# Weight buffers of a float32 decoder trunk at seven different places modulo 256 bytes

## The chip, the cores and the metric

The kernel runs on one core of a Trainium2 chip. A core has TensorE (PE in the profile; PEld is its loading of the stationary operand), VectorE (DVE), ScalarE (ACT), GpSimd (POOL) and SyncE (SP), which here only issues DMAs. Tiles lie in SBUF: 128 partitions, and along each partition a byte address that is the same for all of them. When this text speaks of the place of a tile, it means that address; "modulo 256" is its remainder. Matmul results lie in PSUM, a separate memory that the change does not touch.

The metric is the device time of one execution in microseconds (us). A profile is one execution recorded by the hardware profiler; its span goes from the first to the last instruction.

## The reference, cut to what matters

Four residual layers on 256 tokens of 1,024 channels, all in float32. Layer i uses the mixer A, B, C, A: gated spatial mixing, dilated attention in three groups, and causal pooling with a linear map by group. Every layer reads a large input projection and an output projection from HBM.

```python
def reference(x, ...):
    for i in range(DEPTH):
        kind, j = i % N_MIXERS, i // N_MIXERS
        h = rms_norm(x, norm_gain[i])
        if kind == 0:
            y = mixer_a(h, a_w_in[j], a_v_gain[j], a_w_s[j], a_b_s[j], a_w_out[j])
        elif kind == 1:
            y = mixer_b(h, b_w_in[j], b_q_gain[j], b_k_gain[j], b_w_out[j])
        else:
            y = mixer_c(h, c_w_in[j], c_w_grp[j], c_scale[j], c_w_out[j])
        x = x + y.astype(x.dtype)
    return x

def mixer_a(h, w_in, v_gain, w_s, b_s, w_out):
    proj = h @ w_in                       # u, v, z of 2,048 columns each
    ...
    y = u * mixed * jax.nn.silu(z)
    return y @ w_out
```

## The kernel before

**Products in three matmuls.** To reach float32 accuracy on a faster type (float32r), each operand is split in a high part (rounded by a ScalarE copy, `hi_of`, L82) and a low part (what is left, a VectorE subtraction, `lo_of`, L85). `mm3` (L75 to L79) then issues three matmuls into the same PSUM tile: high x high (L77), high x low (L78), low x high (L79). Each names a stationary operand first, which is loaded into the array, and a moving one, which streams through it.

**Weights as a stream of units.** The host orders all weights into 272 units of 128 partitions x 1,024 float32 (4,096 bytes a partition), in the order of use. `load_units` (L127) brings unit u by a DMA of SyncE into one of four raw buffers wr. `split_hi` (L137) takes a pair of tiles from the weight pool, one high and one low, and writes the high part; `split_units` (L147) writes the low part, after which the raw buffer is free for the load four units on. There are W_BUFS = 7 pairs, used in turn, and the splits run five units (AHEAD) ahead of the matmuls that read them. `next_unit` hands out unit u as wuh and wul.

**Who reads them.** `proj_tok` (v, z, u of layers A; qk and v01 of B; the first cz of C) keeps h stationary (hTh and hTl, 128 x 128 slices) and lets the weights move, 512 columns at a time: 12 matmuls a unit, called wide below. `proj_out` (wo, all layers) does the same with the layer's result y as the stationary operand: y0, y3 in layers A, yb in B, cy in C. `proj_feat` (bz in B; cz and cx in C) turns the roles: weight slices of 128 columns are stationary and 256 columns of h move, 24 matmuls a unit, called narrow. Layer C's `group` (cg) does that with the pooled differences cd in place of h, and the v2p products of layer B move 256 columns of weights over stationary h. The remaining products, mx in layers A and s and o in B, have no weight unit in them: both operands come from tiles of the layer.

**What sets the order.** Nothing is scheduled by cost: the Python program's order is the order on each engine. Small generator tasks (splits of h, attention steps, the transposes by a matmul with an identity, yp, qt, pt and hp) are woken by `tick`, which the projections call after each step, so they fall between matmuls at fixed places. Each engine waits by semaphores for the tiles that it reads and for the buffers that it overwrites.

**What sets the places.** Tiles lie in SBUF in the order in which pools and tags take room. First the pool of x, hTh, hTl, identity and constants, then the weight pool (four wr, seven high, seven low, each 4,096 bytes), and above it the pool of the layer that runs, taken anew for each layer. Within a tag the buffers follow one another without a gap, so all fourteen weight tiles stand at the same remainder.

Of the kernel before, what the change touches and what calls it, by code (L numbers as in the profile page):

```python
# [11 lines left out]
F32R = mybir.dt.float32r  # L12
# [5 lines left out]
P = 128  # L18
# [3 lines left out]
HALF = 512  # L22
# [14 lines left out]
UNIT = 1024  # L37
RAW_BUFS = 4
W_BUFS = 7
# [9 lines left out]
def hybrid_trunk_kernel(ctx, tc, x, wts, norm_gainT, a_v_gain, a_wsT, a_bsT, b_gl, b_gv, c_scaleT,  # L49
# [5 lines left out]
    wp = ctx.enter_context(tc.tile_pool(name="wp", bufs=1))  # L55
# [15 lines left out]
    def pair(pool, shape, tag, name, bufs):  # L71
        return (pool.tile(shape, F32R, tag=tag + "h", name=name + "h", bufs=bufs),
                pool.tile(shape, F32R, tag=tag + "l", name=name + "l", bufs=bufs))
# [7 lines left out]
    def hi_of(hi, src):  # L81
        nc.scalar.activation(hi, src, AF.Copy)  # L82
# [44 lines left out]
    def load_units(n):  # L127
        while loaded[0] < min(n, n_units):
            u = loaded[0]
            raw = wp.tile([P, 2, HALF], F32, tag="wr", name=f"wr{u}", bufs=RAW_BUFS)  # L130
            nc.sync.dma_start(raw, wts[u].rearrange("p (k n) -> p k n", n=HALF))
            raws.append(raw)
            loaded[0] += 1
# [3 lines left out]
    def split_hi(n):  # L137

        while split[0] < min(n, n_units):
            u = split[0]  # L140
            load_units(u + 1)
            hi, lo = pair(wp, [P, 2, HALF], "w", f"w{u}", W_BUFS)
            hi_of(hi, raws[u])
            units.append((hi, lo))
            split[0] += 1

    def split_units(n):  # L147

        split_hi(n)
        while lowered[0] < min(n, n_units):  # L150
            u = lowered[0]
            lo_of(units[u][1], raws[u], units[u][0])
            lowered[0] += 1
            load_units(u + 1 + RAW_BUFS)
# [8 lines left out]
    def step(i, ahead=AHEAD):  # L163

        tick()
        if i % 2 == 0:
            split_hi(used[0] + ahead)
        else:
            split_units(used[0] + ahead)
# [120 lines left out]
    def proj_out(layer, nkt, yT):  # L290
# [15 lines left out]
        for t in range(2):  # L306
            for i, (j, n, w) in enumerate(tail):
                for kk in range(2):
                    k = 2 * j + kk
                    mm3(acc[t][n], yT(k, t), (w[0][:, kk], w[1][:, kk]), False, k == nkt - 1)  # L310
                if t == 0 and nkt == 16 and i == 0:
                    split_units(used[0] + 3)
                if t == 0 and nkt != 16 and i == 2:
                    split_units(used[0] + 1)
                    split_hi(used[0] + 3)
                if t == 1 and i == 0:
                    split_units(used[0] + 4)
                if j == nkt // 2 - 1:
                    xh = xt[t][:, n * HALF:(n + 1) * HALF]
                    nc.vector.tensor_tensor(xh, acc[t][n], xh, op=ALU.add)  # L320
                    if layer == DEPTH - 1:
                        nc.sync.dma_start(out[t * P:(t + 1) * P, n * HALF:(n + 1) * HALF], xh)
                    elif t == 0:
                        half_ss(t, n, ss[t])
                if layer < DEPTH - 1 and i == 3:
                    if t == 0:
                        split_units(used[0] + 2)
                        spawn(norm_task(layer + 1, 0, ss))
                        split_units(used[0] + 3)
                    else:  # L330
                        for n in range(2):
                            half_ss(1, n, ss[1])
                tick()
# [712 lines left out]
```

## Time and profile before

| | |
|---|---|
| time, median of 2 runs | 850.48 us (850.07 and 850.89) |
| the profiled execution's own time | 850.76 us |
| its span | 849.1 us |
| granted TensorE clock, mean | 1.00 |
| DMA share of 16 engines, weight queue | 51.4% |
| HBM read | 147.72 MB |

The profiled execution lies 0.28 us above the median and its time 1.7 us above its span. In a row of the timeline stand the start in us, the duration in us, the engine, the line, the operation, the output, the operands, the shape and how many instructions the row holds. In a row of a group stand the line, the engine, the operation, output and operands with their shapes, the count, the busy time in us and the mean in ns, and then the idle time ahead of these instructions with what ended it. A matmul's duration overlaps that of the next one, so the interval between starts is what it costs in a stream.

Where the tiles stood modulo 256, from the built program (u is the number of the unit):

```
tile                                   before   after
x, ident, kc (v gain, w_s, masks)      128      128
wr (raw weights), hTh, hTl             0        0
wuh and wul, unit u                    0        32 * (u mod 7)
tiles of layers A: v, y, wsr, sz, yy   0        224
tiles of layer B: qk, p, pT, v01, yb   0        224
layer C: cd, szT, czs                  128      96
layer C: cy, cdd, cyy                  0        224
```

### The profile page before, as it was taken

What the parts mean: (1) busy time and instruction counts of PE and PEld (TensorE: products, weight loads), DVE (VectorE), ACT (ScalarE), POOL (GpSimd) and SP (SyncE); (2) the same over time, 40 slices, a digit from 0 to 9 for tenths busy, and PEclk for the clock granted to TensorE, in tenths of its full rate; (3) what the DMA queues carried; (4) which work ended last, traced back from release to release, by engine and by line L of the source; (5) the groups of instructions that cost most, each with busy time, mean ns of one, the idle gap of its engine ahead of it and who ended that gap; (6) DMA issues with size and microseconds to landing.
All of it is one profiled execution on the core that took longest, in us unless ns stands there. A gap on an engine that the chain in (4) does not pass through costs nothing.

```text
span 849.1 us, 12424 instructions
## 1 busy us (share of the span) xinstructions
PE 837.2 (99%) x4600; PEld 724.6 (85%) x4600; DVE 546.8 (64%) x932; ACT 488.9 (58%) x918; POOL 57.4 (7%) x79
## 2 busy tenths in 40 slices
PE   8999999999999999999999999999999999999998
PEld 6888888888988888888888889999988888888886
DVE  6876556646747567667667575797764777555551
ACT  7665444436668677677677566455443676434340
POOL 1301000001001011021021012000000000000000
PEclk9999999999999999999999999999999999999999
DMA  8766565562755346345345268447564376555541
GB/s 286 280 205 222 188 198 172 175 198 96 246 163 166 110 140 193 110 145 187 113 148 181 68 224 261 163 149 248 174 215 157 125 241 208 171 175 173 172 150 50
DMA packets 41500, 149.57 MB, mean 176 GB/s; under 512 B 4864, under 2 KB 4880, under 8 KB 41184
## 3 DMA queue, kind: packets, MB, share of 16 engines
q1 hardware_dynamic: 40320, 144.72, 51.4%
q0 software_dynamic: 976, 4.05, 1.5%
q8 instruction: 36, 0.59, 0.3%
q14 instruction: 24, 0.20, 0.1%
q10 hardware_dynamic: 144, 0.02, 0.0%
HBM read 147.72 MB, written 1.05 MB: 175 GB/s over the span
## 4 chain that ended last, share of the span: by engine, by line
PE 86%; ACT 7%; DVE 2%; issue 2%; POOL 2%; DMA 1%; SPq 0%; POOLq 0%; DVEq 0%
PE wo L77 6%; PE wo L79 6%; PE wo L78 6%; PE qk L77 4%; PE qk L78 4%; PE qk L79 4%; PE z L77 3%; PE z L79 3%; PE z L78 3%; PE u L77 3%; PE u L78 3%; PE u L79 3%; PE v L78 3%; PE v L79 3%; PE v L77 3%; ACT junk L499 2%
## 5 line engine op out<-in xcount | busy, mean ns | idle before, releaser
L504 POOL TENSOR_TENSOR qr<-qm,m 128x4 f32<-128x4 f32 x24 | 30.3, 1272 | 225.4 <-DVE qm L503 225.4
L508 ACT ACTIVATE qn<-qk,qr 128x128 f32<-128x128 f32 x96 | 27.5, 382 | 15.1 <-POOL qr L504 15.1
L499 ACT ACTIVATE junk<-qk 128x128 bf16<-128x128 f32 x96 | 26.8, 279 | 7.2 <-PE qk L79 4.5
L422 DVE TENSOR_TENSOR sz<-u,sz 128x512 f32<-128x512 f32 x16 | 11.0, 686 | 28.0 <-PE u L79 28.0
L225 ACT ACTIVATE hTh<-hp,gT 128x128 fp32r<-128x128 f32 x64 | 17.5, 382 | 16.0 <-PE hp L221 16.0
L206 POOL TENSOR_TENSOR r<-ms,m 128x1 f32<-128x1 f32 x8 | 5.4, 669 | 288.5 <-DVE ms L204 288.5
L320 DVE TENSOR_TENSOR x<-wo,x 128x512 f32<-128x512 f32 x16 | 11.0, 689 | 20.0 <-PE wo L79 20.0
L228 DVE SCALAR_TENSOR_TENSOR hTl<-hp,gT,hTh 128x128 fp32r<-128x128 f32 x64 | 17.9, 343 | 7.7 <-ACT hTh L225 7.7
L364 ACT ACTIVATE junk<-v 128x512 bf16<-128x512 f32 x16 | 9.6, 600 | 17.6 <-PE v L79 17.5
L499 ACT ACTIVATION_READ_ACCUMULATOR junk<-qk 128x1 f32 x96 | 19.1, 199 | 0.0
L365 DVE TENSOR_TENSOR vv<-v,kc 128x512 f32<-128x512 f32 x16 | 10.9, 689 | 12.1 <-ACT junk L364 12.0
L517 DVE TENSOR_TENSOR ra<-qn,kcb 128x64 f32<-128x64 f32 x48 | 10.6, 221 | 12.0 <-ACT qn L508 10.9
L448 ACT ACTIVATE sz<-z 128x512 f32<-128x512 f32 x16 | 9.5, 598 | 15.3 <-PE z L79 14.8
L529 PE MATMUL qt<-ident,qn 128*128 128x128 f32 x96 | 14.6, 274 | 3.5 <-DVE qk22l L537 0.6
L529 PEld LDWEIGHTS qt<-ident,qn 128*128 128x128 f32 x96 | 11.3, 140 | 7.3 <-issue 2.7
L199 ACT ACTIVATE junk<-x 128x512 bf16<-128x512 f32 x16 | 10.3, 643 | 10.7 <-DVE x L320 9.4
L425 DVE SCALAR_TENSOR_TENSOR yy<-mx,bs,sz 128x256 f32<-128x256 f32 x32 | 14.0, 480 | 0.6
L599 ACT ACTIVATE p<-p,rl 128x384 f32<-128x384 f32 (+1 forms) x16 | 11.5, 769 | 4.7 <-DVE rl L598 4.7
L521 DVE TENSOR_TENSOR rb<-qn,kcb 128x32 f32<-128x32 f32 x96 | 13.7, 184 | 0.0
L595 ACT ACTIVATE p<-p,nb 128x768 f32<-128x768 f32 x8 | 7.5, 939 | 8.0 <-DVE nb L594 8.0
L503 DVE TENSOR_SCALAR qm<-qs 128x4 f32<-128x4 f32 x24 | 3.3, 164 | 12.7 <-ACT junk L499 12.7
L345 POOL TENSOR_SCALAR_AFFINE_SELECT kc<-kc 128x128 f32<-128x128 f32 x16 | 9.8, 649 | 14.4 <-DMA kc<-in_a_wsT_dram 8.6
(2770 smaller groups left out, 3269.2 us busy)
## 6 DMA issues: line engine op xcount, KB each, us to landing
wr<-in_wts_dram SPq DMA_DIRECT2D x272, 512.0 KB, 3.8
kc<-in_a_v_gain_dram POOLq DMA_DIRECT2D x2, 1024.0 KB, 6.6
x<-in_x_dram SPq DMA_DIRECT2D x4, 256.0 KB, 4.8
kc<-in_a_wsT_dram POOLq DMA_DIRECT2D x2, 512.0 KB, 8.3
out_dram<-x SPq DMA_DIRECT2D x4, 256.0 KB, 2.0
kcb<-in_masks_dram POOLq DMA_DIRECT2D x1, 576.0 KB, 8.3
kcb<-in_b_gl_dram POOLq DMA_DIRECT2D x1, 192.0 KB, 6.2
kcb<-in_rope_dram POOLq DMA_DIRECT2D x1, 64.0 KB, 8.1
```

Source lines behind the costliest of these rows:

```text
L77: nc.tensor.matmul(out_ap, lh[0], rh[0], start=start, stop=False, skip_group_check=True)
L78: nc.tensor.matmul(out_ap, lh[0], rh[1], start=False, stop=False, skip_group_check=True)
L79: nc.tensor.matmul(out_ap, lh[1], rh[0], start=False, stop=stop, skip_group_check=True)
L225: nc.scalar.activation(hTh[:, k, sl], pts[k // 4][:, k % 4], AF.Copy, scale=gT[:, layer, k:k + 1])
L228: nc.vector.scalar_tensor_tensor(hTl[:, k, sl], pts[k // 4][:, k % 4], gT[:, layer, k:k + 1], hTh[:, k, sl].bitcast(F32), op0=ALU.mult, op ...
L425: nc.vector.scalar_tensor_tensor(y[:, sl], mxs[n][t][:, sl], bsT[:, 2 * n + gg:2 * n + gg + 1], us[t][:, sl], op0=ALU.add, op1=ALU.mult)
L499: nc.scalar.activation(junk[:, :HD], ov[t][:, h], AF.Square, accum_out=ssq[t][:, h:h + 1])
L504: nc.gpsimd.tensor_tensor(rq[t], ms, m05, op=ALU.pow)
L508: nc.scalar.activation(qn[t][:, h], ov[t][:, h], AF.Copy, scale=rq[t][:, h:h + 1])
L521: nc.vector.tensor_tensor(rb[:, hs, s0:s0 + 16], qn[t][:, hs, s1:s1 + 16], c, op=ALU.mult)
L529: nc.tensor.transpose(pts[t][:, h], qn[t][:, h], ident)
L599: nc.scalar.activation(f, f, AF.Copy, scale=rl[i][:, 0:1])
```

## The change

In `split_hi` the call of `pair` with the tag "w" and seven buffers is replaced by two tiles with tags of their own for each of the seven places ("wh0", "wl0" to "wh6", "wl6"), one buffer each. The low tile is 8 float32 (32 bytes) longer than the unit, and the code uses the first 1,024 elements of both.

```diff
             u = split[0]
             load_units(u + 1)
-            hi, lo = pair(wp, [P, 2, HALF], "w", f"w{u}", W_BUFS)
+            hi, lo = [wp.tile([P, UNIT + pad], F32R, tag=f"w{part}{u % W_BUFS}", name=f"w{u}{part}",
+                              bufs=1)[:, :UNIT].rearrange("p (k n) -> p k n", n=HALF)
+                      for part, pad in (("h", 0), ("l", 8))]
             hi_of(hi, raws[u])
             units.append((hi, lo))
```

A pair now takes 4,096 + 4,128 = 8,224 bytes, which is 32 more than a multiple of 256, so the pairs follow one another at remainders 0, 32, 64, 96, 128, 160 and 192, the high and the low tile of a unit at the same one. The weight pool grows by 7 x 32 = 224 bytes, and each layer pool begins 224 bytes further on. Everything allocated ahead of the weight tiles stays where it was.

The instructions are the same in number, shape and order on every engine, and every wait has the same semaphore and value as before. Unit u takes the place that unit u - 7 had, as before.

## The prediction

> **What bounds the kernel now.** I read the page's busy times first, then its slices and chain, then a table by stage, and last single rows of TensorE's timeline, since only those show the interval from one matmul to the next.
>
> ```profile
> span 849.1 us, 12424 instructions
> PE 837.2 (99%) x4600; PEld 724.6 (85%) x4600; DVE 546.8 (64%) x932; ACT 488.9 (58%) x918; POOL 57.4 (7%) x79
> PEclk9999999999999999999999999999999999999999
> PE 86%; ACT 7%; DVE 2%; issue 2%; POOL 2%; DMA 1%; SPq 0%; POOLq 0%; DVEq 0%
> ```
>
> TensorE is busy 99% of the span, the clock is granted in full throughout, and the chain that ended last runs 86% through matmuls. The table by stage shows where something else is waited for:
>
> ```profile
> 100.00:200.00 100.00, 100.00 (x469) 83.25 (x468) 55.85 (x70) 42.24 (x57) 1.07 (x2) 1.00 0.52 171
> 300.00:400.00 100.00, 97.91 (x534) 83.45 (x533) 69.90 (x183) 77.57 (x208) 13.58 (x10) 1.00 0.48 155
> 600.00:700.00 100.00, 100.00 (x513) 85.66 (x512) 65.56 (x86) 55.86 (x86) 1.11 (x2) 1.00 0.56 186
> ```
>
> The columns after the stretch and its length are PE, PEld, DVE, ACT and POOL busy, the clock, the DMA share and GB/s. Outside the first 20 us and the attention layer (2.1 us idle in 300 to 400) the matmul stream never stops. So the time is the number of matmuls times their interval. "Busy" does not tell that interval, because neighbouring matmuls overlap; starts do:
>
> ```profile
> 39.64 0.39 PE L77 MATMUL v<-w10h,hTh 128*128 128x512 f32 x1
> ...
> 55.96 0.39 PE L77 MATMUL z<-w16h,hTh 128*128 128x512 f32 x1
> ...
> 523.67 0.28 PE L77 MATMUL cx<-hTh,w160h 128*128 128x256 f32 x1
> ...
> 526.55 0.28 PE L77 MATMUL cx<-hTh,w161h 128*128 128x256 f32 x1
> ```
>
> From unit 10 to unit 16 lie 6 units of 12 wide matmuls (512 columns): 16.32 us / 72 = 226.7 ns. Unit 160 is 24 narrow ones (256 columns): 2.88 / 24 = 120.0 ns. Twice the columns cost 106.7 ns more, so 0.417 ns a column and 120.0 - 106.7 = 13.3 ns besides, in both. That surplus of 13.3 ns is the only thing on the path that the place of a buffer could reach.
>
> **The change, part by part.** It adds no instruction, takes none away, and leaves every queue's order, every wait and every semaphore value as they were; the second operand tile of each pair is 32 bytes longer, and things move in SBUF. Modulo 256 bytes, unit u now lies at 32 x (u mod 7), and every tile of the layer pools lies 224 further (224 bytes are allocated below them). hTh, hTl, x, the raw weight buffers wr and the constants stay. Four costs follow.
>
> *DMA.* The 272 weight loads go to wr, which does not move; v gain, w_s, masks and x stay too. Only the small csc and rcn of layer C move. Cost 0; even if those two were late, layer C needs them tens of microseconds after their issue.
>
> *VectorE and ScalarE.* They write and read the moved tiles. Rows on tiles that are off the 256-byte grid already:
>
> ```profile
> L365 DVE TENSOR_TENSOR vv<-v,kc 128x512 f32<-128x512 f32 x16 | 10.9, 689 | 12.1 <-ACT junk L364 12.0
> L422 DVE TENSOR_TENSOR sz<-u,sz 128x512 f32<-128x512 f32 x16 | 11.0, 686 | 28.0 <-PE u L79 28.0
> L782 DVE TENSOR_TENSOR nx<-xc 128x542 f32<-128x542 f32 x8 | 5.7, 718 | 6.8 <-ACT xc L775 6.8
> L775 ACT ACTIVATE xc<-cx 128x512 f32<-128x512 f32 x8 | 4.7, 594 | 10.6 <-PE cx L79 10.2
> L764 ACT ACTIVATE szT<-cz 128x512 f32<-128x512 f32 x6 | 3.6, 598 | 6.3 <-PE cz L79 6.0
> ```
>
> kc lies at 128, sz at 0: 689 against 686 ns. nx works on slices shifted by one element: 718 ns for 542 elements, 29 ns more than 689 for 512, which is the 30 elements at the ordinary rate. xc is written 64 bytes past its tile's start: 594 against 598. So 0, from -4 to +4 ns an operation. What would hide a slower split is the five units that ScalarE and VectorE run ahead, and their idle 42% and 36%; without that cover, 272 splits at 4 ns on two engines are 2 us.
>
> *Narrow matmuls.* Before, moving and stationary operand stand at the same place modulo 256 in all of them but one group, the products of layer C's groups (cg), whose moving cd lies 128 further than the weights:
>
> ```profile
> 558.23 0.28 PE L77 MATMUL cg<-cd3h,w172h 128*128 128x256 f32 x1
> 558.35 0.28 PE L78 MATMUL cg<-cd3l,w172h 128*128 128x256 f32 x1
> ...
> 563.93 0.28 PE L77 MATMUL cz<-hTh,w174h 128*128 128x256 f32 x1
> ```
>
> 48 matmuls in 5.70 us: 118.75 ns, 1.25 less than the cx rows of the same size, form and stationary tiles. This is the only row in which the offset between the operands differs, and it differs in time: places do matter a little. Now the offset changes in 168 of bz (24 of 192 keep 0), 240 of cz (of 288), 312 of cx (of 384) and all 192 of v2p. 912 x -1.25 = -1.1 us. A quarter of cg's 192 come to offset 0 and lose the gain: +0.06. mx, s and o have both operands in the layer pool, which moves as one: 0.
>
> *Wide matmuls.* 2,640 of them, and 2,340 get an offset: all 672 of wo (w at 32 x (u mod 7), y at 224, so never equal), and six of seven units elsewhere. No wide row of before has an offset, so I bound it. Upper end: after a block of transposes the wide matmuls lose their even interval for ten to twelve starts, and then find it again:
>
> ```profile
> 81.91 0.60 PE L433 MATMUL yp<-ident,yy 128*128 128x128 f32 x4
> 82.26 0.49 PE L77 MATMUL z<-w25h,hTh 128*128 128x512 f32 x1
> 82.59 0.39 PE L78 MATMUL z<-w25l,hTh 128*128 128x512 f32 x1
> ...
> 83.05 0.40 PE L77 MATMUL z<-w25h,hTh 128*128 128x512 f32 x1
> 83.28 0.40 PE L78 MATMUL z<-w25l,hTh 128*128 128x512 f32 x1
> 83.52 0.39 PE L79 MATMUL z<-w25h,hTl 128*128 128x512 f32 x1
> ...
> 84.90 0.39 PE L79 MATMUL z<-w25h,hTl 128*128 128x512 f32 x1
> ```
>
> 82.59 to 84.90 is 10 intervals of 231.0, +4.3 on the even 226.7; two in a row (83.05 to 83.52) reach 235, +8.3. Lower end: the surplus goes altogether, -13.3. Between these the value nearest to a wide matmul at the same engine clock and in an undisturbed stretch is 226.7 itself: in cg the offset moved the surplus by 1.25 of 13.3 and in a form whose matmul lasts about as long as its weight load; a wide one lasts twice as long and has slack there. I take 0.
>
> Sum against the profiled execution (850.76 us, span 849.1 and 1.7 around it): 850.76 - 1.1 + 0.06 = 849.7. The median shown is 850.48, 0.28 below that execution, so 849.4.
>
> The Trainium skill, SBUF — State Buffer, section "Specifications (TRN2)", gives lines of 16 bytes and a penalty for each crossing into a new one. All steps of 32 bytes keep whole lines, so by that rule alone the sum would be 0 and the time 850.5. The trace differs from it by the 1.25 ns of cg, whose 128 bytes are whole lines as well.
>
> **The rivals.**
>
> *Slower: the wide matmuls lose their even interval for good.* For it: cg, with an offset, never settles at 120.0 as cx does, and unsettled wide rows run at 231.0. Against it: unsettled cg was faster, not slower. Price: the transposes are
>
> ```profile
> L529 PE MATMUL qt<-ident,qn 128*128 128x128 f32 x96 | 14.6, 274 | 3.5 <-DVE qk22l L537 0.6 <-DVE qk12l L537 0.6 <-DVE qk32l L537 0.5
> L630 PE MATMUL pt<-ident,p 128*128 128x128 f32 x48 | 9.9, 274 | 0.0
> L433 PE MATMUL yp<-ident,yy 128*128 128x128 f32 x64 | 9.6, 271 | 0.0
> L221 PE MATMUL hp<-ident,xs 128*128 128x128 f32 x64 | 8.4, 274 | 0.4 <-DVE xs L212 0.3
> L628 PE MATMUL pt<-ident,p 128*128 128x128 f32 x24 | 6.2, 276 | 0.0
> ```
>
> in blocks of four (yp, qt), eight (hp) and three or four (pt), about 68 places, each followed by about ten unsettled matmuls, so some 600 of 2,340 pay already. 1,740 x 4.3 = +7.5, time 856.9; with all 2,340 counted 859.4. It would be slower by over 2% from +17 us, 7.3 ns on each of 2,340, which only a stage at the 235 of the row pair reaches: 849.4 + 2,340 x 8.3 = 868.8.
>
> *The wide ones gain as cg did.* 2,340 x -1.25 = -2.9, time 846.5; with twice that on all 3,252 shifted matmuls, 842.4. For it: cg. Against it: the slack just named.
>
> *The surplus is a clash of the two operands' reads and the offset removes it.* 3,252 x -13.3 = -43, time 807; half of it 828. Against it: cg is offset and keeps 12.1 of 13.3. The Trainium skill, TensorE: Matmul & The Clock Gate, section "Wait — 56ns, not 53.3ns?", has a fixed 2.5 ns besides the columns in back-to-back matmuls at full clock, which leaves 10.8 of the 13.3 unexplained; by that the time would fall to about 815. The trace has 13.3 in both sizes and no row of 2.5.
>
> *Nothing moves at all*, because cg's 1.25 has another cause: 850.5. For it: 1.25 ns is one row's difference. Against it: all four cg groups stand beside cx and cz rows that keep 120.0.
>
> **How the numbers follow.** Chances: narrow alone, 849.4 (own range 847 to 852), 0.40; wide unsettled, about 857, 0.27; wide gain, 842 to 847, 0.15; nothing, 850.5, 0.08; wide near 235, about 869, 0.05; surplus much reduced, 807 to 830, 0.05. Forecast 849.4. The range runs from 842 (gain on all shifted) to 861 (all wide ones unsettled, 859.4, and a little of the engines' 2 us); the last two cases stay outside, with the tails of the others about 2 in 10. Two per cent, about what a measurement of this kernel tells from no change, are 17 us: faster 0.05, same 0.90, slower 0.05.
>
> **What would show it.** In the profile after, cx and cz units with u a multiple of 7 (161, 168) should keep 120.0 and their neighbours fall to about 119. Wide rows of v with u = 7, 14 are a control at 226.7; if their neighbours read 231, the slower rival holds, if 225 the faster. wo has no control unit and would show the effect most. The durations of the splits (L82, L85) and the waits of TensorE should not change. I am wrong if the wide interval depends on the offset, since 2,340 matmuls turn 1 ns into 2.3 us.

## The result, and the profile after

The kernel with seven places takes 859.41 us (859.19 and 859.63), the one before 850.48 us: a ratio of 1.0104, 95% interval 1.0084 to 1.0125. It is slower by 8.9 us. That lies inside the range of the prediction, 842 to 861, but its forecast of 849.4 was for a gain.

The page of the kernel after, its span, busy times, granted clock and chain:

```profile
span 857.9 us, 12424 instructions
PE 846.5 (99%) x4600; PEld 722.5 (84%) x4600; DVE 546.9 (64%) x932; ACT 488.8 (57%) x918; POOL 55.5 (6%) x79
PEclk9999999999999999999999999999999999999999
PE 86%; ACT 7%; DVE 2%; issue 2%; POOL 2%; DMA 1%; SPq 0%; POOLq 0%; DVEq 0%
```

The same instructions, the same clock, VectorE and ScalarE as busy as before to 0.1 us, and TensorE busy for 9.3 us longer. No new wait has come in: TensorE is without work for 11.4 us of the span, where it was 11.9. The table by stage of the kernel after (columns as in the prediction) shows the same from another side:

```profile
100.00:200.00 100.00, 100.00 (x461) 81.65 (x460) 54.38 (x62) 39.11 (x47) 0.56 (x1) 1.00 0.52 172
300.00:400.00 100.00, 98.96 (x524) 83.03 (x523) 67.32 (x181) 76.21 (x214) 15.58 (x12) 1.00 0.46 148
```

From 100 to 200 us TensorE never stops in either kernel, but starts 461 matmuls where it started 469. So each takes longer. Which ones, the timeline of the kernel after tells, at the first matmul of units 8 to 16:

```profile
34.93 0.40 PE L77 MATMUL v<-w8h,hTh 128*128 128x512 f32 x1
37.73 0.40 PE L77 MATMUL v<-w9h,hTh 128*128 128x512 f32 x1
40.49 0.40 PE L77 MATMUL v<-w10h,hTh 128*128 128x512 f32 x1
43.30 0.40 PE L77 MATMUL v<-w11h,hTh 128*128 128x512 f32 x1
...
51.70 0.39 PE L77 MATMUL v<-w14h,hTh 128*128 128x512 f32 x1
54.46 0.40 PE L77 MATMUL v<-w15h,hTh 128*128 128x512 f32 x1
57.26 0.40 PE L77 MATMUL z<-w16h,hTh 128*128 128x512 f32 x1
```

Twelve wide matmuls lie between two rows. Unit 8 (32 bytes from h) takes 2.80 us, 233 ns each; unit 9 (64) 2.76, 230; unit 10 (96) 2.81, 234. Unit 14 stands at 0, as h does, and takes 2.76, 230: not 226.7, because it comes out of a stream that has lost its even interval and needs about the whole unit to find it again. Only its last two intervals, 227 and 226 ns by the trace, are the even ones. The narrow ones went the other way (units 160 to 163 of the kernel after, 24 matmuls each):

```profile
528.58 0.28 PE L77 MATMUL cx<-hTh,w160h 128*128 128x256 f32 x1
...
531.40 0.28 PE L77 MATMUL cx<-hTh,w161h 128*128 128x256 f32 x1
...
534.27 0.28 PE L77 MATMUL cx<-hTh,w162h 128*128 128x256 f32 x1
...
537.11 0.28 PE L77 MATMUL cx<-hTh,w163h 128*128 128x256 f32 x1
```

Unit 160 takes 117.5 ns a matmul, 161 (distance 0) 119.6, 162 118.3 (the rows are rounded, so each is good to about 0.4), where all took 120.0. Means and sums over all matmuls of each trace that are followed at once by the next one (within 260 ns a wide one, within 160 a narrow one):

```
                                before              after               difference
wide (512 columns), 2,558       227.90 ns           232.39 ns           +11.5 us
narrow (256 columns), 1,468     119.60 ns           118.41 ns            -1.75 us
all other time of TensorE       84.6 us             83.7 us              -0.9 us
span                            849.1 us            857.9 us             +8.8 us
```

(The first two differences are the count times the change of the mean; the third row is what is left between TensorE's first and last start.) That accounts for the whole: the wide matmuls lost 11.5 us, the narrow ones gave 1.75 back, and the rest of TensorE's time was 0.9 shorter.

### The profile page after: what moved, and what is told of

Read it like the earlier page. It is cut to its first block, busy times and chain, and to the rows that moved or that the text cites. A ratio compares the mean times of both kernels' runs of the same rounds, so it can differ in the third digit from the quotient of the medians.

```text
span 857.9 us, 12424 instructions
## 1 busy us (share of the span) xinstructions
PE 846.5 (99%) x4600; PEld 722.5 (84%) x4600; DVE 546.9 (64%) x932; ACT 488.8 (57%) x918; POOL 55.5 (6%) x79
## 4 chain that ended last, share of the span: by engine, by line
PE 86%; ACT 7%; DVE 2%; issue 2%; POOL 2%; DMA 1%; SPq 0%; POOLq 0%; DVEq 0%
PE wo L77 6%; PE wo L79 6%; PE wo L78 6%; PE qk L77 4%; PE qk L79 4%; PE qk L78 4%; PE z L77 3%; PE z L79 3%; PE u L79 3%; PE z L78 3%; PE u L77 3%; PE u L78 3%; PE v L78 3%; PE v L79 3%; PE v L77 3%; ACT junk L501 2%
## 5 line engine op out<-in xcount | busy, mean ns | idle before, releaser
L227 ACT ACTIVATE hTh<-hp,gT 128x128 fp32r<-128x128 f32 x64 | 17.5, 382 | 16.5 <-PE hp L223 16.5
L601 ACT ACTIVATE p<-p,rl 128x384 f32<-128x384 f32 (+1 forms) x16 | 11.5, 768 | 4.7 <-DVE rl L600 4.7
L777 ACT ACTIVATE xc<-cx 128x512 f32<-128x512 f32 x8 | 4.7, 595 | 10.3 <-PE cx L79 10.0
```

The source lines that it names most:

```text
L227: nc.scalar.activation(hTh[:, k, sl], pts[k // 4][:, k % 4], AF.Copy, scale=gT[:, layer, k:k + 1])
L601: nc.scalar.activation(f, f, AF.Copy, scale=rl[i][:, 0:1])
```

## The experiments

In what follows the distance is the place of the moving operand less that of the stationary one, modulo 256 bytes. The theory after the result: the interval follows this distance. Against it stood three others: that a tile off a 256-byte boundary costs by itself; that it is the variety, a distance that changes from unit to unit, which keeps the stream from settling; and that other engines' writes disturb it.

**Everything moved together.** One edit ahead of all tiles moves weights, h, raw buffers and layer pools by 96 bytes; the distances stay as they were.

```diff
-    xt = [cp.tile([P, D], F32, tag=f"x{t}", name=f"x{t}") for t in range(2)]
+    xt = [cp.tile([P, D + 24 * (1 - t)], F32, tag=f"x{t}", name=f"x{t}")[:, :D] for t in range(2)]
```

> Everything from the second x tile on lies 96 bytes further than before: weights, h, raw buffers and layer pools together, so moving and stationary operand keep equal remainders (96 and 96), as before (0 and 0). Theory 'distance' (the interval follows the distance between the two operands modulo 256): wide matmuls 226.7 ns, narrow 120.0, cg 118.8, time as before, 850.5 us within 1. Rival 'boundary' (a moving tile off a 256-byte boundary costs, whatever the other one does): wide about 234 as the kernel after shows for units at 96, some +16 us, about 866. Rival 'other engines' (splits written off the boundary disturb the stream): slower too, 855 or more.

Measured: 850.74 us (10 runs, 850.46 to 851.06) beside 850.73 for the kernel before on the same chip, ratio 1.000 (0.9991 to 1.001). Its timeline, units 10 and 16, 160 and 161:

```profile
39.96 0.39 PE L77 MATMUL v<-w10h,hTh 128*128 128x512 f32 x1
...
56.28 0.39 PE L77 MATMUL z<-w16h,hTh 128*128 128x512 f32 x1
...
523.95 0.28 PE L77 MATMUL cx<-hTh,w160h 128*128 128x256 f32 x1
...
526.83 0.28 PE L77 MATMUL cx<-hTh,w161h 128*128 128x256 f32 x1
```

16.32 us over 72 and 2.88 over 24: 226.7 and 120.0, to the digit. The boundary theory and that of the other engines, as stated, fall: here the weights, h, the tiles of the layers, every split and every load of weights stand off the boundary. Since all moved together, this run alone can't tell whether it matters that others write at another remainder than TensorE reads; the surveys can.

**Only the layer pools moved.** The weight tiles take tags of their own without any pad, and 56 floats behind the last one move the layer pools by 224 bytes.

```diff
-            hi, lo = pair(wp, [P, 2, HALF], "w", f"w{u}", W_BUFS)
+            b = u % W_BUFS
+            hi, lo = [wp.tile([P, pre + UNIT + post], F32R, tag=f"w{part}{b}", name=f"w{u}{part}",
+                              bufs=1)[:, pre:pre + UNIT].rearrange("p (k n) -> p k n", n=HALF)
+                      for part, pre, post in (("h", 0 if b == 0 else 0, 0),
+                                              ("l", 0, 56 if b == W_BUFS - 1 else 0))]
```

> The weight tiles stay at remainder 0; only the layer pools lie 224 further, as in the kernel after. Distance: only wo gets one (weights 0, y 224, so 32): its 672 wide matmuls go from about 227.5 to 233, +3.7 us, cg from 118.8 to about 120 (+0.2), all else as before: 854.4 us. Boundary: the moving weights stand at 0, wo stays at 227, time 850.5. Rival 'variety' (the stream does not settle because the distance changes from unit to unit): the distance is constant in wo, so 226.7 and 850.5.

Measured: 854.41 us, ratio 1.0044 (1.0027 to 1.0061); forecast 854.4. The wide rows of v as before, those of wo (units 54 and 60) not:

```profile
40.23 0.39 PE L77 MATMUL v<-w10h,hTh 128*128 128x512 f32 x1
...
56.55 0.39 PE L77 MATMUL z<-w16h,hTh 128*128 128x512 f32 x1
...
170.08 0.39 PE L77 MATMUL wo<-w54h,y01h 128*128 128x512 f32 x1
...
186.88 0.39 PE L77 MATMUL wo<-w60h,y03h 128*128 128x512 f32 x1
```

72 matmuls in 16.32 us and 72 in 16.80: 226.7 at distance 0 and 233.3 at distance 32, in one run. The moving weights stand on the boundary in both. The distance in wo is constant, and it did not settle at 226.7, so variety is not needed.

**All units at one place.** The same edit with 24 floats ahead of the first weight tile and 40 behind the last: all seven pairs at 96, the layer pools at 0.

> All seven pairs at the same remainder 96, h and layer pools at 0 as before. Distance: every wide matmul at 96, about 234 instead of 227.9 on the mean, 2640 x 6.1 = +16 us; narrow ones at 160, about 118.5, 864 x -1.4 = -1.2: about 865 us. Variety: the distance never changes, so the stream settles, 226.7, 850.5 us. Boundary: 865 too.

Measured: 861.2 us, ratio 1.0124 (1.0109 to 1.0139). Units 10 and 16:

```profile
40.35 0.40 PE L77 MATMUL v<-w10h,hTh 128*128 128x512 f32 x1
...
57.15 0.40 PE L77 MATMUL z<-w16h,hTh 128*128 128x512 f32 x1
```

16.80 us / 72 = 233.3 ns. Variety falls as the main cause: with one constant distance the kernel is slower than with seven. The size was 4 us off, mostly because at a constant 96 the wide matmuls average 233.2 and not the 234.2 that unit 10 shows among changing neighbours, so at this place the change of distance itself seems to cost about 1 ns. The 1,468 narrow ones came to 118.4.

**Two surveys.** Blocks of four units (two in layer C) at chosen remainders, six pairs for room.

```diff
-W_BUFS = 7
+W_BUFS = 6
...
-            hi, lo = pair(wp, [P, 2, HALF], "w", f"w{u}", W_BUFS)
+            blk = u // 2 if 152 <= u < 208 else u // 4
+            at = (0, 112, 224, 80, 192, 48, 160, 16, 128, 240, 96, 208, 64, 176, 32, 144)[blk % 16] // 4
+            hi, lo = [wp.tile([P, UNIT + 64], F32R, tag="w" + part, name=f"w{u}{part}",
+                              bufs=W_BUFS)[:, at:at + UNIT].rearrange("p (k n) -> p k n", n=HALF)
+                      for part in ("h", "l")]
```

> Units in blocks of four (two in layer C) at remainders 0 to 240 in steps of 16, tiles one after another at 0 (six pairs instead of seven, for room). Distance: each remainder has its own interval, the same in v, z, u, qk and wo: 226.7 at 0, about 233, 230, 234, 232.7, 233.5, 232.8, 232.8 at 32, 64, ... 224, whatever the neighbours are; odd multiples of 16 between these or near them. Variety: inside each block of 48 the stream settles at 226.7. Time about 860, which decides nothing.

> As the first survey (six pairs, blocks of four units, two in layer C), at distances from -28 to 40 in steps of 4 bytes. If the distance counts by the byte, wide intervals climb between the known ones: 226.7 at 0, 231.7 at 16, 233.2 at 32, 236 at 240. If only whole 16-byte lines count, 4, 8 and 12 read as 0 does, 226.7, and 244, 248 and 252 as 240. If any distance but 0 unsettles the stream, 4 bytes already give 230 or more.

The second has the remainders 0, 4, 252, 8, 244, 12, 28, 248, 20, 236, 24, 228, 16, 36, 240, 40. They took 872.71 and 872.24 us (one execution each), where about 860 was expected of the first. With six pairs TensorE is without work for 19.4 and 19.6 us in place of 11.9, so their times are not compared with the others; the intervals are what they were made for. Four blocks of 48 in the second one, at distances 4, 252, 8 and 244:

```profile
23.47 0.40 PE L77 MATMUL v<-w4h,hTh 128*128 128x512 f32 x1
...
34.88 0.40 PE L77 MATMUL v<-w8h,hTh 128*128 128x512 f32 x1
...
45.82 0.40 PE L77 MATMUL v<-w12h,hTh 128*128 128x512 f32 x1
...
57.01 0.40 PE L77 MATMUL z<-w16h,hTh 128*128 128x512 f32 x1
...
68.51 0.40 PE L77 MATMUL u<-w20h,hTh 128*128 128x512 f32 x1
```

11.41, 10.94, 11.19 and 11.50 us: 237.7, 227.9, 233.1 and 239.6 ns. Means over all starts that had twelve matmuls of the same size and distance ahead of them, in ns, for most of the distances in both surveys (0: the kernel before; some rest on one unit of twelve starts):

```
distance        0     4     8     12    16    20    28    32    48    64    80    96
wide            226.7 237.8 232.9 228.9 231.7 238.3 227.2 233.3 233.3 229.0 231.1 233.3
narrow          120.0 120.1 118.0 119.9 117.4 -     119.0 116.7 116.7 117.7 118.2 120.1

distance        112   128   144   160   176   192   208   224   240   244   248   252
wide            231.1 232.2 233.3 234.4 233.0 233.4 234.5 233.4 236.4 239.5 232.0 227.8
narrow          120.0 118.6 119.9 117.3 118.9 -     118.4 118.3 118.5 116.6 115.5 118.3
```

Four bytes are enough to cost 11 ns, while 12, 28 and 252 cost 0.5 to 2.2, so neither the byte count nor whole lines order the table. Distances that differ by 256 or 512 read alike. No wide distance tried beats 0; for the narrow ones 0 is among the worst.

In v, z, u, qk and wo the same distance gives the same interval to within 1.4 ns, with one exception: at 240, unit 251 of z runs evenly at 233.3, where wo, v and u run at about 236.7. Narrow matmuls differ more: at 28, cx has 120.1 and v2p 115.9, at 8 cz has 117.4 and v2p 120.0. The distance is thus the main term and not the only one. It is TensorE's own operands that count: the splits run five units ahead and so write at the remainders of other blocks, yet units 17, 18 and 19, all at 244, have 240.0 each while those writes pass from one block to the next.

**High and low tiles apart.** High weight tiles at 0, low ones at 64.

> High weight tiles at 0, low ones at 64; all else as before. In a wide product the second of three matmuls then moves a tile at distance 64, the other two at 0; in a narrow one the third loads a stationary tile at 192. If each matmul pays for its own pair: wide L78 about 230 and L77, L79 226.7 (880 x 3.2 = +2.8 us), narrow L79 114 to 118 (288 x -4 = -1.2), about 852 us. If a mixture unsettles the whole stream: all three lines alike, 230 to 233, 856 to 862 us.

Measured: 857.85 us (one execution). Its timeline at unit 12:

```profile
45.72 0.40 PE L77 MATMUL v<-w12h,hTh 128*128 128x512 f32 x1
45.96 0.40 PE L78 MATMUL v<-w12l,hTh 128*128 128x512 f32 x1
46.19 0.39 PE L79 MATMUL v<-w12h,hTl 128*128 128x512 f32 x1
46.42 0.40 PE L77 MATMUL v<-w12h,hTh 128*128 128x512 f32 x1
46.66 0.39 PE L78 MATMUL v<-w12l,hTh 128*128 128x512 f32 x1
46.89 0.39 PE L79 MATMUL v<-w12h,hTl 128*128 128x512 f32 x1
```

All three lines are spread alike; over wo the means are 231.3 (L77), 232.2 (L78) and 232.5 (L79). A matmul does not pay for its own pair alone: one of three at a distance unsettles the whole stream, to 232.0 over all wide ones, more than the 229.0 of a constant 64. The second branch of the expectation holds.

**A version that uses it.** The weights stay at 0. Layer C, which is nearly all narrow, writes its h and cd at another remainder.

```diff
-    hTh = cp.tile([P, KT, S], F32R, tag="hTh", name="hTh")
-    hTl = cp.tile([P, KT, S], F32R, tag="hTl", name="hTl")
+    hT = [cp.tile([P, KT * S + 64], F32R, tag=f"hT{p}", name=f"hT{p}") for p in "hl"]
+    h_at = [0, 0, 8, 0]
+
+    def h_of(layer):
+        return [t[:, h_at[layer]:h_at[layer] + KT * S].rearrange("p (k s) -> p k s", s=S) for t in hT]
...
-            dh, dl = pair(pl, [P, 4, S], "cd", f"cd{g}", 2)
+            dh, dl = [a[:, 40:40 + 4 * S].rearrange("p (k s) -> p k s", s=S)
+                      for a in pair(pl, [P, 4 * S + 64], "cd", f"cd{g}", 2)]
```

At 192 and at 248 bytes the 8 becomes 48 and 62, and the 40 of cd becomes 16 and 30.

> The kernel before, with h of layer C and cd written 32 bytes past their former remainder of the weights (both at 32, weights at 0); layers A and B as before. Distance: cx and cz narrow at 32, 116.8 instead of 120 (624 narrow and 48 more: 672 x -3.2 = -2.2 us), cg 192 x -2 = -0.4, the first cz of layer C wide at 224, 48 x 5.4 = +0.3: 848.4 us, ratio 0.997. Boundary or variety: no gain, 850.7 or more.

> The same with h of layer C and cd at 192. In the kernel after, narrow matmuls at 192 ran at 114.0 to 114.4 in cz and bz and at 118 in cx; so cx and cz gain 2 to 6 ns on 672 (-1.3 to -4.0 us), cg 1 to 4 on 192, the wide cz at 64 loses 48 x 2: 846 to 849.5 us.

> As the version with layer C's moving tiles at 32, now at 248. The second survey read 115.75 ns there in one block of 48 narrow matmuls, the lowest of all. Distance: cx and cz 672 x -4.2 = -2.8 us, cg 192 x -3 = -0.6, the first wide cz at distance 8, 48 x 5 = +0.2: 847.5 us, ratio 0.9963. If that block was a chance orbit, as 114 at 192 was, anything between 847.5 and 849.5.

At 32: 848.44 us (9 runs, 847.88 to 848.68) beside 850.70 for the kernel before on the same chip, ratio 0.9973 (0.9963 to 0.9983); forecast 848.4. At 192: 848.92, ratio 0.9976 (0.9968 to 0.9985), with one execution of eleven at 845.45. At 248: 851.61 beside 850.64, ratio 1.001 (1.0001 to 1.0019), outside all that was expected of it. From unit 160 to unit 172, 288 narrow matmuls, in the timelines of the three, in this order:

```profile
523.88 0.28 PE L77 MATMUL cx<-hTh,w160h 128*128 128x256 f32 x1
...
557.48 0.28 PE L77 MATMUL cg<-cd3h,w172h 128*128 128x256 f32 x1
```

```profile
523.07 0.28 PE L77 MATMUL cx<-hTh,w160h 128*128 128x256 f32 x1
...
556.99 0.28 PE L77 MATMUL cg<-cd3h,w172h 128*128 128x256 f32 x1
```

```profile
523.71 0.28 PE L77 MATMUL cx<-hTh,w160h 128*128 128x256 f32 x1
...
558.27 0.28 PE L77 MATMUL cg<-cd3h,w172h 128*128 128x256 f32 x1
```

33.60, 33.92 and 34.56 us: 116.7, 117.8 and 120.0 ns. The first is what the survey said. The third is not: the survey's 115.5 at 248, a single block, did not come back. So a distance allows more than one repeating pattern: 192 showed 114.0 in the cz rows of the kernel after, 118.0 in its cx rows and 117.8 here. What decides which one comes is not shown; that it is how the stream enters is a guess. The one execution at 845.45 would fit the 114 pattern, but its trace was not taken.

## Why the prediction was wrong

*What bounds the kernel, and that only the surplus of 13.3 ns could move.* Right: the change lies in the matmul intervals, all but the 0.9 us that the rest of TensorE's time gave back.

*DMA and the other engines: 0.* Right. The 272 splits average 1,061 ns on ScalarE in both kernels, and 1,222 and 1,223 on VectorE; unit 9's low part, from 0 to 64, in the groups before and after:

```profile
L85 DVE TENSOR_TENSOR w9l<-wr,w9h 128x1024 fp32r<-128x1024 f32 x1 | 1.3, 1303 | 0.0
```

```profile
L85 DVE TENSOR_TENSOR w9l<-wr,w9h 128x1024 fp32r<-128x1024 f32 x1 | 1.3, 1305 | 0.0
```

*Narrow matmuls: -1.1 us.* Right in sign, mis-sized: -1.75. The step took cg's 1.25 ns for every distance; in the survey 32, 64 and 160 give 2.3 to 3.3, and 96 gives nothing.

*Wide matmuls: 0.* This is the step that failed. The prediction bounded it by -13.3 and +8.3 and then took 0, on the ground that a wide matmul "lasts twice as long and has slack there". The runs refute that: at a constant distance of 32 or 96 the wide interval is 233.3, so +6.6 a matmul, where the narrow one changes by -3.3 and 0. Over the kernel it came to +4.5 on each of 2,558, +11.5 us. The slack itself can be looked up, for each of the 4,600 matmuls has its weight load (PEld) in the trace, in the same order. The load for the first matmul of unit 10, in the kernel before and with all units at 96:

```profile
39.42 0.19 PEld L77 LDWEIGHTS v<-w10h,hTh 128*128 128x128 f32 x1
```

```profile
40.12 0.19 PEld L77 LDWEIGHTS v<-w10h,hTh 128*128 128x128 f32 x1
```

The matmuls start at 39.64 and 40.35. Over the wide streams a load takes 187.7 ns in the one kernel and 187.8 in the other, and ends 37 and 43 ns ahead of its matmul. So the room was there and grew, the load was no longer, and the interval rose all the same: the error was to conclude from room behind the load that the distance can't count. (For the narrow matmuls the record has the load of 191 ns, longer than their interval of 120, end some 74 ns after their start. So a recorded end is not the moment at which a matmul could begin, and the records don't tell where the 6.6 ns go.)

*The slower rival.* It named the place, and its price was close: 856.9, or 859.4 with all 2,340 counted, against 859.41. That the second hits the measured time is luck: it adds 4.3 on 2,340 wide matmuls (10.1 us) to -1.1 us for the narrow ones, where the runs have 11.5 us on 2,558 wide ones, -1.75 on the narrow ones and -0.9 elsewhere. Its mechanism was half right. The wide stream does lose its even interval, as after transposes, but the distance sets a level of its own, mostly above the 231.0 that the prediction read from the unsettled rows. In hindsight the one row with a distance, cg, spoke for it more than the 0.27 allows: it never settled at an even interval, and that carried over to the wide ones, while the sign of its mean did not.

*The wide ones gain as cg did.* Refuted: no wide distance tried lies below 226.7.

*The surplus as a clash that a distance removes, and the 16-byte lines.* Refuted for the wide matmuls, whose lowest settled interval is the one at 0. The narrow ones do lose part of the 13.3 ns, 3.3 at distance 32 and 6 in the cz rows of 114.0, but never all of it. The Trainium skill's 2.5 ns besides the columns (TensorE: Matmul & The Clock Gate, "Wait — 56ns, not 53.3ns?") is shown by no distance here; the least is about 7, in those cz rows. The 16-byte lines of the Trainium skill (SBUF — State Buffer, section "Specifications (TRN2)") do not order the wide intervals either: 240, on whole lines, costs 10 ns in most rows, while 28, which begins inside a line, costs 0.5.

*The control.* Units 7 and 14, at distance 0, were to stay at 226.7; they ran at 230.2. Twelve matmuls are about as many as the stream needs to settle, as the rows after transposes had shown. The forecast for wo, where the effect was to be largest, held: 227.5 to 232.8 ns on the mean, +5.3, where the other wide products rose by 3.2 to 4.9.

## What to carry to other kernels

Where a stream of float32r matmuls bounds the time, read the start-to-start interval from the timeline and compare it by shape; a busy share of 99% hides 2%. Keep the places of moving and stationary tiles apart by a multiple of 256 bytes when 512 columns move, and try another distance for 256 columns (32 gave 116.7 against 120.0 here, worth 2.3 us); pads between pools change it silently. When the only row with some property behaves unlike all the others, ask what it did, not only in which direction its mean went.

## What the runs showed of the hardware

In these streams a float32r matmul's interval depends on the distance between its operands modulo 256 bytes, down to 4 bytes, and not on the place that both share: 96 bytes on both changed 0.01 us.

The averages of settled streams fall on multiples of 6.667 ns or simple fractions of them: 226.67 is 34, 233.33 is 35, 120.0 is 18, 116.67 is 17.5. In the kernel before, 3,061 of the 3,074 evenly spaced starts (those with the next one 226 or 227 ns later, or 120 for narrow ones) fall into the same 2.5 ns of a grid of 6.667 ns over the whole span. Within an even stretch that follows from the interval; that the stretches after an interruption come back to the same place of the grid does not, so the even interval looks like a lock onto something that runs at that period. Which part of the chip that is, and why the distance decides which averages are possible, stays open: the runs vary places, not the array's reads of its two operands, and the recorded weight loads keep their length of 188 ns when the wide interval goes from 226.7 to 233.3.
